# Two-layer hybrid encoder: memory values of the second layer split from an SBUF copy, memory key heads transposed and split later, rotation tables made from the twelfth slot on

## The chip, the core and the metric

The kernel runs on one core of one Trainium2 chip. The core has a matrix engine (TensorE, PE in the profile), a vector engine (VectorE, DVE), an activation engine (ScalarE, ACT), a general engine (GpSimd, POOL), and a queue for DMA issues (SyncE, SP). Each engine runs its own instructions strictly in the order in which the program lists them; between engines they wait for semaphores. The metric is device time of one execution in microseconds (us), lower is better.

## What is computed

```python
for i in range(DEPTH):                       # 2 layers, 512 tokens, width 1024
    h = rmsnorm(x, norm_g[i])
    mem_h = rmsnorm(mem, mem_norm_g[i])      # 256 memory tokens
    proj = jnp.einsum('bsd,de->bse', h, w_in)
    ...
    o_mem = memory_attention(q_mem, mem_h, w_mem_kv[i], mem_qn_g[i], mem_kn_g[i])
    y = jnp.concatenate([o_mix, o_mem], axis=-1) * jax.nn.silu(gate)
    x = x + jnp.einsum('bse,ed->bsd', y, w_out[i])

def memory_attention(q_mem, mem_h, w_kv, qn_g, kn_g):
    ...
    kv = jnp.einsum('bnd,de->bne', mem_h, w_kv).reshape(Bn, N, 2, MEM_HEADS, HEAD_DIM)
    k = rmsnorm(kv[:, :, 0], kn_g)
    v = kv[:, :, 1]
    s = jnp.einsum('bqhe,bkhe->bhqk', q, k).astype(jnp.float32)
    p = jax.nn.softmax(s, axis=-1).astype(v.dtype)
    return jnp.einsum('bhqk,bkhe->bqhe', p, v).reshape(Bn, S, MEM_W)
```

Layer 0 mixes tokens by dilated window attention, layer 1 by grouped-query attention whose queries and keys are turned by 2-D axial rotary tables. All arithmetic is in float32.

## The kernel before

**Three products for one.** A float32 matrix product is made of products of halves: an operand is cast to the type fp32r (the high half), and the rest, operand minus high half, is the low half. High times high, high times low and low times high are added up in PSUM. So everything that PE multiplies is first cast (mostly on ScalarE) and then subtracted (mostly on VectorE): two instructions on two engines, the second of which reads the first's result. For weights these are the lines 313 (`wh`) and 323 (`wo`), for the activations of the second layer 573 and 574.

**Seven products for eight.** `s_chunk` makes each block of 512 output columns in seven products instead of eight block products, with sums of the weights (in this layer all made by DMAs that add, issued on POOL, lines 278 to 297) and sums of the activations. The seven, in order: 12, 11, S1, S2, S4, S3, 22. Their activations, `h12`, `h11`, `hS1`, `hS2`, `hS4`, `hS3`, `h22`, are made at the end of the first layer from the residual stream, in two blocks of 128 tokens each (`diffs_t`, `rest_t`, whose `put` casts at line 573 and subtracts at line 574). PSUM banks are used twice: S2 adds on top of the bank of 11, after the addition at line 405 has read that bank out; S4 on that of 12, S3 on S2's, after a copy by line 388.

**Slots.** The order of work is written out by hand. A *slot* is one group of matmuls (12 of 512 columns in `mem_kv`, 24 of 256 in `s_chunk` here, about 2.9 us). In each slot the program lists: the matmuls of the group; `drv.free()`, the first step of whatever evacuates a bank that is due; `W.advance()`, the weights' work (line 323, a sum on POOL, line 313, loads on SyncE, in that order); `drv.tick()`, which first runs what was marked `soon`, then each waiting generator that is due (`yield n` puts it off by n slots), and then what was marked `late`. An instruction in a tick so stands behind the slot's own matmuls and ahead of those of the next slot.

The stretch around the change is the begin of the second layer. Its slots are called here:

- K1 to K4 and V1 to V4: memory keys and values, `mem_kv(1, ...)`, two halves of the contraction for two blocks of 128 memory tokens. They end about 661 us after the start.
- M1 to M7: the seven products of the memory queries, from 661 to 684.
- C1 to C7: those of the new keys and values, from 684 on; then come those of the queries, the gates, and the output.

The first slot, K1, has number 1, so that V1 is 5, M1 is 9, C1 is 16.

**What the change touches.** In `mem_kv`, `ev_k` squares the keys of a block in their bank (line 598), multiplies them by the reciprocal norm into an SBUF tile (line 603, in V1 and V2), transposes the four heads on PE two slots later (line 610, ticks V3 and V4), and splits the transposed heads in `put_norm`: the high half late in the same tick (line 647, ACT), the low half `LO_K[1]` = 5 slots on, at the begin of ticks M5 and M6 (line 650, DVE). `ev_v` splits the values straight from their bank: high half in V4 and M1 (line 675, ACT), low half at once for the first block and three slots on, in tick M4, for the second (line 678, DVE). `setup_b` loads the rotation tables and two gain rows by three DMAs on SyncE in tick `SET_B` = 9, M1, and multiplies them on VectorE in ticks M5, M6, M7 and C1 (four times line 1373, before the third of which line 1371 scales a gain). The tables are read first in tick C5 (lines 1430, 1431), the memory keys and values in the memory attention, which begins behind C7.

Squares, differences, copies of banks, `xn` and the tables' sources all take tiles of 128 x 512 from one pool of 14 buffers (`s2`). Weight loads (line 262) stand in SyncE's queue in the order in which the slots list them; SyncE runs ahead of the other engines as far as free buffers allow.

Of the kernel before, what the change touches and what calls it, by code (L numbers as in the profile page):

```python
# [10 lines left out]
F32 = mybir.dt.float32  # L11
F32R = mybir.dt.float32r
AF = mybir.ActivationFunctionType
ALU = mybir.AluOpType
# [7 lines left out]
TCKW = {}  # L22
NBIG, NM4, NS2, SCRATCH = 7, 23, 14, 2048
RING, LEAD = 4, 2
BULK, ACTIVE, SET_AT, MEM_B, PREP_Y, PREP_B, HALF, SET_B = 2, 2, 15, 14, 1, 1, {"a": 3, "b": 3, "o": 0}, 9
MEM_STEP = 1, 1
MEM_D = 4
DIRECT, DIRECT_B = (7,), (4, 5, 6, 7)
LO_K, LO_V = (9, 5), (0, 3)
PD = 2  # L30
EO = 2, 2, 1, 2, 2, 1
YB = {"m": (2, 2), "k": (1, 1, 1), 0: (1, 2, 1), 1: (1, 2, 1)}
# [98 lines left out]
def trunk_kernel(ctx: ExitStack, tc: tile.TileContext, x, mem, wall, norm_g, mem_norm_g, gcol,  # L131
                 qn_a, kn_a, qn_b, kn_b, ident_d, mask_d, tab_a, tab_b, out):
    nc = tc.nc
    V, A, G, T = nc.vector, nc.scalar, nc.gpsimd, nc.tensor
# [11 lines left out]
    def m4(dt=F32, name="m4"):  # L146
        return pool.tile([128, 1024], dt, tag="m4", name=name, bufs=NM4)

    def s2(dt=F32, name="s2"):
        return pool.tile([128, 512], dt, tag="s2", name=name, bufs=NS2)  # L150
# [350 lines left out]
    def turn4(src, hi, lo, mid=None):  # L501

        p = at("xT")
        for k in range(4):
            T.transpose(p[:, k * 128:(k + 1) * 128], src[:, k * 128:(k + 1) * 128], ident)
        p = p.rearrange("p (k t) -> p k t", k=4)
        if mid:
            mid()
        if hi is not None:
            split(hi, lo, p)  # L510
        return p
# [10 lines left out]
    def proj_t(act, sels, evac, mid=None):  # L522

        def group(w, u, b, p):
            for k in range(4):
                kk = 4 * u + k
                mm_early(p, sels[b](act, 0, kk), w[k][0], sels[b](act, 1, kk), w[k][0], kk == 0)
            if mid:
                mid(u, b)
            for k in range(4):  # L530
                kk = 4 * u + k
                mm_late(p, sels[b](act, 0, kk), w[k][1], kk == 7)
        chunk(2, len(sels), group, evac)
# [60 lines left out]
    def head_sq(p, n=4, by=QS):  # L594
        ss = sm(n, "hss")
        for j in range(n):
            jk = small.tile([128, 128], F32, tag="junk", name="junk", bufs=2)
            A.activation(jk, p[:, j * 128:(j + 1) * 128], AF.Square, scale=by, accum_out=ss[:, j:j + 1])  # L598
        return rstd_of(ss, n)

    def head_mul(p, r, n=4, dst=None):
        xn = (s2(name="xn") if dst is None else dst).rearrange("p (a b) -> p a b", a=4)
        V.tensor_tensor(xn[:, 0:n], p.rearrange("p (a b) -> p a b", a=4)[:, 0:n],  # L603
                        r[:, 0:n, None].to_broadcast([128, n, 128]), ALU.mult)
        return xn

    def transpose4(xn, n=4):
        p = at("qT")
        for j in range(n):
            T.transpose(p[:, j * 128:(j + 1) * 128], xn[:, j, :], ident)  # L610
        return p.rearrange("p (a b) -> p a b", a=4)
# [33 lines left out]
    def put_norm(q, gain, hi, lo, wait=0):  # L645

        drv.late(lambda: A.activation(hi, q, AF.Copy, scale=gain))
        if wait:
            yield wait
        drv.soon(lambda: V.scalar_tensor_tensor(lo, q, gain, hi.bitcast(F32), ALU.mult, ALU.subtract))  # L650
        yield 1

    def mem_kv(layer, M, mid=None):
        kt_ = [m4(F32R, "kmT").rearrange("p (h t) -> p h t", h=4) for _ in range(2)]
        vt_ = [m4(F32R, "vm").rearrange("p (b e) -> p b e", b=2) for _ in range(2)]

        def ev_k(b, p):
            r = head_sq(p) if layer else head_sq(p, by=rm[:, 2 + b:3 + b])

            def rest():  # L660
                if not layer:
                    G.tensor_scalar(r, r, rm[:, b:b + 1], None, ALU.mult)
                xn = head_mul(p, r)
                yield 2
                q = transpose4(xn)
                cs = slice(b * 128, (b + 1) * 128)
                yield from put_norm(q, gk_m[layer], kt_[0][:, :, cs], kt_[1][:, :, cs], LO_K[layer])

            drv.release(rest(), 2)
            yield 1  # L670

        def ev_v(b, p):

            h = 0.5 if layer else rm[:, 4 + b:5 + b]
            A.activation(vt_[0][:, b], p, AF.Copy, scale=h)
            if b and LO_V[layer]:
                yield LO_V[layer]
            V.scalar_tensor_tensor(vt_[1][:, b], p, h, vt_[0][:, b].bitcast(F32), ALU.mult, ALU.subtract)
            yield 1

        proj_t(M, NAT[:2], ev_k, mid)
        proj_t(M, NAT[:2], ev_v)
        return kt_, vt_

# [352 lines left out]
    p = turn4(mg[0, 0], None, None)  # L1037
# [631 lines left out]
```

## Time and profile before

| | |
|---|---|
| time, median of 3 runs | 953.63 us (952.09 to 953.82) |
| profiled execution | 953.29 us, of which span 951.4 us |
| PE busy | 937.2 us (99%) |
| VectorE busy | 790.0 us (83%) |
| ScalarE busy | 681.1 us (72%) |
| POOL busy | 340.0 us (36%) |
| granted TensorE clock | 1.00 |

How to read the lines that follow. In the stages, a row gives the stretch, its length, and for PE, its weight loads (PEld), DVE, ACT and POOL the busy time in it and the number of instructions, then the granted clock, the mean share of the DMA engines in use and the GB/s moved. In the order of time, a row gives start and length, engine, line, operation, out<-in, shape and count; in brackets how long the engine had been idle and what ended that. In PE's order, matmuls are pipelined and their ends are modelled, so that a row's length overlaps the next start; start to start is what it costs. A tile's rows give minimum, median and maximum in ns, and the first and last start. "DMA to landing" is from issue to the arrival of the data.

### The profile page before, as it was taken

To read this page: it belongs to the slowest core of one execution; us is meant where nothing else is said; L and a number is where in the kernel's file an instruction comes from. 1 tells how busy PE (TensorE), PEld (TensorE's weight loads), DVE (VectorE), ACT (ScalarE), POOL (GpSimd) and SP (SyncE) were. 2 spreads that over 40 slices of the span, in tenths; PEclk is the share of its full clock that TensorE was granted. 3 is DMA by queue.
4 is the path that set the end of the run, shared out by engine and by line. 5 is a ranking of instruction groups with operands and counts; after the bars stand their busy time and mean duration, and the time that the engine had idled before them with its cause. 6 is when DMAs were issued, how large, how long until landed. Compare 5 with 4: busy or idle time off the path is not lost.

```text
span 951.4 us, 16573 instructions
## 1 busy us (share of the span) xinstructions
PE 937.2 (99%) x5680; PEld 830.7 (87%) x5680; DVE 790.0 (83%) x1411; ACT 681.1 (72%) x1698; POOL 340.0 (36%) x484
## 2 busy tenths in 40 slices
PE   8999999999999999999999999999899999999998
PEld 6789888888888888888889998888899999998886
DVE  6997676878888888889798999868978998769982
ACT  7775689676868686868676768457778886878860
POOL 3323323656554545464827011213233241011110
PEclk9999999999999999999999999999999999999999
DMA  9999946869787878696868989979876686776524
GB/s 352 387 252 326 283 97 160 298 118 273 153 254 148 258 154 265 156 266 133 254 169 194 275 202 247 283 275 297 227 166 140 179 237 174 213 201 177 127 57 127
DMA packets 86198, 203.51 MB, mean 214 GB/s; under 512 B 25057, under 2 KB 34529, under 8 KB 86114
## 3 DMA queue, kind: packets, MB, share of 16 engines
q1 hardware_dynamic: 66962, 139.46, 42.9%
q0 software_dynamic: 17856, 60.83, 34.3%
q10 hardware_dynamic: 1296, 2.16, 0.6%
q8 instruction: 45, 0.74, 0.3%
q14 instruction: 39, 0.32, 0.1%
HBM read 156.48 MB, written 11.34 MB: 176 GB/s over the span
## 4 chain that ended last, share of the span: by engine, by line
PE 90%; DVE 4%; ACT 2%; DMA 2%; issue 1%; POOL 0%; SPq 0%; DVEq 0%; ACTq 0%; POOLq 0%
PE pj L176 24%; PE pj L175 24%; PE pj L179 24%; PE qT L610 2%; PE sa L1189 2%; PE oo L1297 2%; PE pt L1276 1%; PE ptb L1499 1%; DVE wo L323 1%; PE sa L1185 1%; PE ob L179 1%; DMA odb<-o 1%; PE pmt L735 1%; DMA m<-in_mem_dram 1%; PE ob L176 1%
## 5 line engine op out<-in xcount | busy, mean ns | idle before, releaser
L323 DVE TENSOR_TENSOR wo<-wl,wh 128x1024 fp32r<-128x1024 f32 x255 | 315.0, 1241 | 6.3 <-ACT wh L313 5.9
L313 ACT CAST wh<-wl 128x1024 fp32r<-128x1024 f32 x255 | 268.8, 1060 | 32.9 <-PE pj L176 19.2
L175 PE MATMUL pj<-wh,hS 128*128 128x512 f32 (+1 forms) x448 | 157.4, 365 | 1.7 <-DVE sn L405 1.7
L176 PE MATMUL pj<-wh,hS 128*128 128x512 f32 (+1 forms) x448 | 152.2, 353 | 0.6 <-DVE hS L574 0.6
L175 PE MATMUL pj<-wh,h 128*128 128x512 f32 (+1 forms) x336 | 117.8, 364 | 0.0
L176 PE MATMUL pj<-wh,h 128*128 128x512 f32 (+1 forms) x336 | 114.1, 353 | 1.1 <-DVE h L574 1.1
L453 POOL TENSOR_TENSOR rstd<-mse,half 128x4 f32<-128x4 f32 (+2 forms) x96 | 101.4, 1056 | 8.0
L179 PE MATMUL pj<-wo,hS 128*128 128x512 f32 (+1 forms) x448 | 99.9, 352 | 0.0
L175 PEld LDWEIGHTS pj<-wh,hS 128*128 128x128 f32 x448 | 84.8, 189 | 12.1 <-DVE sn L405 2.1
L176 PEld LDWEIGHTS pj<-wh,hS 128*128 128x128 f32 x448 | 84.9, 190 | 11.0 <-DVE hS L574 0.8
L179 PEld LDWEIGHTS pj<-wo,hS 128*128 128x128 f32 x448 | 74.7, 189 | 11.8
L452 POOL TENSOR_SCALAR mse<-hss 128x4 f32<-128x4 f32 (+1 forms) x86 | 42.6, 495 | 112.9 <-ACT junk L598 108.5
L388 ACT COPY sn<-pj 128x512 f32<-128x512 f32 x116 | 64.5, 590 | 24.0 <-PE pj L179 23.2
L1133 POOL TENSOR_TENSOR ta<-sn,tabs 128x128 f32<-128x128 f32 (+1 forms) x64 | 39.8, 629 | 116.6 <-DVE sn L603 91.1
L598 ACT ACTIVATE junk<-sn 128x128 f32<-128x128 f32 x264 | 79.2, 309 | 1.2 <-DVE sn L399 1.2
L179 PE MATMUL pj<-wo,h 128*128 128x512 f32 (+1 forms) x336 | 74.8, 352 | 0.0
L176 PEld LDWEIGHTS pj<-wh,h 128*128 128x128 f32 x336 | 63.7, 190 | 8.8 <-DVE h L574 1.3
L175 PEld LDWEIGHTS pj<-wh,h 128*128 128x128 f32 x336 | 63.6, 189 | 7.3
L405 DVE TENSOR_TENSOR sn<-pj,sn 128x512 f32<-128x512 f32 x87 | 59.6, 686 | 8.5 <-PE pj L179 8.1
L297 POOL DMA_DIRECT2D wl<-wl x33 | 29.5, 903 | 103.7 <-DVE wo L323 54.5
L179 PEld LDWEIGHTS pj<-wo,h 128*128 128x128 f32 x336 | 56.0, 189 | 8.8
L287 POOL DMA_DIRECT2D wl<-wl x33 | 31.3, 976 | 72.7 <-DVE wl L282 21.4
(252 smaller groups left out, 2363.6 us busy)
## 6 DMA issues: line engine op xcount, KB each, us to landing
wl<-in_wall_dram SPq DMA_DIRECT2D x222, 512.0 KB, 7.4
wl<-wl POOLq DMA_DIRECT2D x66, 512.0 KB, 6.2
wl<-in_wall_dram POOLq DMA_DIRECT2D x42, 512.0 KB, 8.6
od<-o SPq DMA_DIRECT2D x11, 256.0 KB, 5.7
og<-od SPq DMA_DIRECT2D x10, 256.0 KB, 9.4
x<-in_x_dram SPq DMA_DIRECT2D x4, 512.0 KB, 9.0
v0d<-sn SPq DMA_DIRECT2D x8, 256.0 KB, 8.4
acc<-in_x_dram POOLq DMA_DIRECT2D x8, 256.0 KB, 6.4
```

The costliest lines, as they stand in the source:

```text
L175: T.matmul(o, a, b, start=start, stop=False, skip_group_check=True)
L176: T.matmul(o, c, d, start=False, stop=False, skip_group_check=True)
L179: T.matmul(o, a, b, start=False, stop=stop, skip_group_check=True)
L287: G.dma_start(self.tile[key], self.tile[c, "T1", x], accum_op=ALU.add)
L313: A.copy(wh, self.tile[self.items[i]])
L323: V.tensor_tensor(wo, self.tile[key], wh.bitcast(F32), ALU.subtract)
L388: A.copy(t, b)
L405: V.tensor_tensor(t, b, t, ALU.subtract if q == "12" else ALU.add)
L452: G.tensor_scalar(e, ss, EPS, None, ALU.add)
L453: G.tensor_tensor(r, e, half[:, 0:n], ALU.pow)
L598: A.activation(jk, p[:, j * 128:(j + 1) * 128], AF.Square, scale=by, accum_out=ss[:, j:j + 1])
L1133: G.tensor_tensor(ta[:, 0:n], xn[:, 0:n, 0:32], ropeA[:, 0, b, s0:s0 + n], ALU.mult)
```

## The change

The first layer is left as it is. In the second layer:

- **Values.** ScalarE copies the scaled bank to an `s2` tile (`vr`) where it used to write the high half (V4 and M1). The high half is cast from that copy on ScalarE `HI_V` = 6 slots on (ticks M6 and M7), and the low half is subtracted on VectorE two slots behind that (ticks C1 and C2), now by a plain subtraction of two SBUF tiles. It adds one ScalarE instruction for each of two blocks.
- **Keys.** The transposes wait 6 slots instead of 2 (ticks M3 and M4 instead of V3 and V4), and with them the high halves; the low halves come 4 slots behind that instead of 5, at the begin of ticks C1 and C2 instead of M5 and M6.
- **Tables.** `SET_B` is 12 instead of 9: the three loads are issued in tick M4, and the products are made in ticks C1 to C4.

```diff
-BULK, ACTIVE, SET_AT, MEM_B, PREP_Y, PREP_B, HALF, SET_B = 2, 2, 15, 14, 1, 1, {"a": 3, "b": 3, "o": 0}, 9
+BULK, ACTIVE, SET_AT, MEM_B, PREP_Y, PREP_B, HALF, SET_B = 2, 2, 15, 14, 1, 1, {"a": 3, "b": 3, "o": 0}, 12
...
-LO_K, LO_V = (9, 5), (0, 3)
+LO_K, TURN_K, HI_V, LO_V = (9, 4), (2, 6), 6, (0, 2)
...
                 xn = head_mul(p, r)
-                yield 2
+                yield TURN_K[layer]
                 q = transpose4(xn)
...
         def ev_v(b, p):
 
             h = 0.5 if layer else rm[:, 4 + b:5 + b]
-            A.activation(vt_[0][:, b], p, AF.Copy, scale=h)
-            if b and LO_V[layer]:
+            if layer:
+                t = s2(name="vr")
+                A.activation(t, p, AF.Copy, scale=h)
+                yield HI_V
+                A.copy(vt_[0][:, b], t)
                 yield LO_V[layer]
-            V.scalar_tensor_tensor(vt_[1][:, b], p, h, vt_[0][:, b].bitcast(F32), ALU.mult, ALU.subtract)
+                V.tensor_tensor(vt_[1][:, b], t, vt_[0][:, b].bitcast(F32), ALU.subtract)
+            else:
+                A.activation(vt_[0][:, b], p, AF.Copy, scale=h)
+                V.scalar_tensor_tensor(vt_[1][:, b], p, h, vt_[0][:, b].bitcast(F32), ALU.mult, ALU.subtract)
             yield 1
```

## The prediction

> **What bounds the kernel now.** I read the page first, then the stages, then PE's, VectorE's and ScalarE's order of time around the change.
>
> ```profile
> span 951.4 us, 16573 instructions
> PE 937.2 (99%) x5680; PEld 830.7 (87%) x5680; DVE 790.0 (83%) x1411; ACT 681.1 (72%) x1698; POOL 340.0 (36%) x484
> 670.00:680.00 10.00, 8.77 (x71) 8.56 (x72) 10.00 (x15) 7.37 (x18) 3.09 (x4) 1.00 0.98 270
> 680.00:690.00 10.00, 8.94 (x75) 8.74 (x74) 9.86 (x15) 5.81 (x15) 2.56 (x3) 1.00 0.72 160
> ```
>
> TensorE (PE) is the bound, at a granted clock of 1.00: it is idle for 951.4 - 937.2 = 14.2 us, and only idle time on it can be won. In the two stages shown it idles 1.23 + 1.06 us, while VectorE (DVE) has not a free microsecond. These are M3 to M7, where the change works. The PE rows there:
>
> ```profile
> 660.65 0.60 PE L610 MATMUL qT<-ident,xn 128*128 128x128 f32 x4
> 661.01 0.36 PE L175 MATMUL pj<-wh,h 128*128 128x256 f32 x1
> ...
> 670.66 0.39 PE L175 MATMUL pj<-wh,hS 128*128 128x256 f32 x1 [0.79 <-DVE sn L405]
> ...
> 673.64 0.28 PE L175 MATMUL pj<-wh,hS 128*128 128x256 f32 x1
> ...
> 676.52 0.28 PE L175 MATMUL pj<-wh,hS 128*128 128x256 f32 x1
> ...
> 678.33 0.39 PE L176 MATMUL pj<-wh,hS 128*128 128x256 f32 x1 [0.57 <-DVE hS L574]
> ...
> 680.23 0.28 PE L175 MATMUL pj<-wh,h 128*128 128x256 f32 x1
> ...
> 682.53 0.39 PE L176 MATMUL pj<-wh,h 128*128 128x256 f32 x1 [1.06 <-DVE h L574]
> ...
> 684.43 0.28 PE L175 MATMUL pj<-wh,h 128*128 128x256 f32 x1
> ...
> 692.54 1.12 PE L179 MATMUL pj<-wo,hS 128*128 128x256 f32 x8
> ```
>
> M4 starts at 670.66, M5 at 673.64, M6 at 676.52, M7 at 680.23, C1 at 684.43. M5 runs undisturbed in 2.88 us. M4 waits for the addition that empties its bank (L405); M6 takes 3.71 and M7 4.20, because each waits halfway for the low half of its own activations (L574). All three waits end on VectorE. Its queue:
>
> ```profile
> L678 DVE SCALAR_TENSOR_TENSOR vm<-pj,vm x2: 683/686/689, 663.3 to 674.0; 128x512 fp32r<-128x512 f32 x2
> ```
>
> In order of time (start, length, and in brackets the idle time before it with its releaser):
>
> ```profile
> 665.84 0.69 DVE L574 TENSOR_TENSOR hS<-f,hS 128x512 fp32r<-128x512 f32 x1 [0.69 <-ACT hS L573]
> ...
> 669.92 0.69 DVE L405 TENSOR_TENSOR sn<-pj,sn 128x512 f32<-128x512 f32 x1
> ...
> 676.33 0.75 DVE L650 SCALAR_TENSOR_TENSOR kmT<-qT,gc,kmT 128x512 fp32r<-128x512 f32 x1
> 676.99 0.69 DVE L1373 TENSOR_TENSOR tabs<-tbraw,grB 128x512 f32<-128x512 f32 x1
> 677.59 0.69 DVE L574 TENSOR_TENSOR hS<-fS,hS 128x512 fp32r<-128x512 f32 x1
> ...
> 679.92 0.75 DVE L650 SCALAR_TENSOR_TENSOR kmT<-qT,gc,kmT 128x512 fp32r<-128x512 f32 x1
> ...
> 681.78 0.69 DVE L574 TENSOR_TENSOR h<-f,h 128x512 fp32r<-128x512 f32 x1
> ...
> 683.52 0.23 DVE L1371 TENSOR_SCALAR grB<-grB 128x128 f32<-128x128 f32 x1
> ...
> 687.53 1.22 DVE L323 TENSOR_TENSOR wo<-wl,wh 128x1024 fp32r<-128x1024 f32 x1
> ...
> 690.90 0.69 DVE L405 TENSOR_TENSOR sn<-pj,sn 128x512 f32<-128x512 f32 x1 [0.88 <-PE pj L179]
> ```
>
> Ahead of the three late instructions stand memory values (L678), memory keys (L650) and the rotation tables (L1373), none of which is used before C5. One of 512 elements takes 0.60 from start to start (676.99 to 677.59), an L650 0.66 (676.33 to 676.99). ScalarE (ACT), which feeds the L574s:
>
> ```profile
> 661.93 0.69 ACT L647 ACTIVATE kmT<-qT,gc 128x512 fp32r<-128x512 f32 x1
> 662.51 0.59 ACT L675 ACTIVATE vm<-pj 128x512 fp32r<-128x512 f32 x1
> ...
> 673.85 0.59 ACT L388 COPY sn<-pj 128x512 f32<-128x512 f32 x1
> 674.33 1.05 ACT L313 CAST wh<-wl 128x1024 fp32r<-128x1024 f32 x1
> 675.28 0.63 ACT L573 CAST hS<-fS 128x512 fp32r<-128x512 f32 x1
> ...
> 680.43 0.59 ACT L388 COPY sn<-pj 128x512 f32<-128x512 f32 x1 [3.06 <-PE pj L179]
> ```
>
> **M4: values' low half out of the way.** The first L678 (663.3) moves behind M7, so VectorE is 0.60 ahead. The idle 0.69 before 665.84 waits for a ScalarE cast; that cast comes earlier too, since an L647 leaves ScalarE in front of it (0.58, 661.93 to 662.51). The chain to L405 has no other gap: it runs at 669.32, and M4 starts at 670.06 instead of 670.66. PE itself would be ready earlier: 670.66 - 0.79 = 669.87, less 0.36 for the head transposes of which one pair, not two, now lies before M4 (660.65 to 661.01), gives 669.51. So M4 still waits for VectorE, about 0.55. Gain 0.60; the second head's 0.36 is still to be paid: 0.24.
>
> **M6.** M5 starts at 670.06 + 2.98 (M4's 670.66 to 673.64) + 0.36 = 673.40, M6 at 676.28. M6 ran dry 1.24 after its start (678.33 - 0.57 - 676.52), so it now needs its low half at 677.52. VectorE loses from its queue between 669.92 and 677.59 an L678, an L650 and an L1373, 1.86, and could be there at 675.13. It is not: ScalarE is now later. The key heads' copies (L647) run after M3 and M4; the second one needs transposes that start after M4 (673.04) and end 0.60 on, so it runs at 673.7. Then L388 at 674.28, L313 0.48 later, the cast 0.95 after that, 675.71, done at 676.33. L574 runs 676.38 to 677.07. M6 does not wait, with 0.45 to spare: gain 3.71 - 2.88 = 0.83.
>
> **M7.** It starts at 679.16 and needs its low half 1.24 later (682.53 - 1.06 - 680.23), at 680.40. From one L574 to the other VectorE took 4.19 (677.59 to 681.78), with an L650 and an L1373 in between; without them 2.93: 679.31 to 680.00. Gain 4.20 - 2.88 = 1.32, with 0.4 to spare. Sum at C1: 0.24 + 0.83 + 1.32 = **2.39 us**; C1 starts at 682.04.
>
> **Added copies.** A copy of values from SBUF on ScalarE isn't shown as such; the cast of an activation from SBUF (0.63, 675.28) is the same shape and is taken. Two of them stand in ticks M6 and M7, where ScalarE idles 3.06 before 680.43 and 4.2 of the ten from 680 (5.81 busy): nothing. Without that cover they would cost about 0.6 each. The copy that takes the place of L675 reads PSUM as L675 did (0.59). The values' low half now reads SBUF alone; L574, which does so too, and L678, from PSUM, both take 0.69, so I take no difference.
>
> **What is paid back in C1 to C4.** Before, VectorE came to the L405 that frees C4's bank at 690.90 after 0.88 idle, so it was free at 690.02. Now, between the L574 of M7 (2.47 earlier) and that L405 stand two L650 and two value subtractions more and one L1371 less: 2 x 0.66 + 2 x 0.60 - 0.26 (683.52 to the next table) = 2.26; of the tables two stand there before and after. It runs at 690.02 - 2.47 + 2.26 = 689.81 and is done at 690.50. C4 started some 0.96 after the row at 692.54, 693.50, and now at 691.11. It does not wait; the cover is 0.6 us, where it was 1.9. What is late next: L1371 and the last two tables, 0.26 + 2 x 0.60 = 1.46 more in C3 and C4. No PE instruction of these slots reads what stands behind them, and the first reader of a table is in C5. I take 0; the bound is 1.5, were PE to wait for all of it.
>
> **SyncE's queue.** The three table loads move from tick M1 to M4, past three weight loads. Its longest wait for the first of them, then seven weight loads and two of POOL's, each with its time to landing:
>
> ```profile
> SPq L1364 <- ACT sq L492: 4.3, 1, 4.3
> ...
> L262 SPq DMA_DIRECT2D wl<-in_wall_dram x7: 327/328/849, 651.1 to 660.8; - x7
> DMA to landing us min/median/max: 9.6/16.1/18.0
> ...
> 661.97 1.05 POOL L278 DMA_DIRECT2D wl<-in_wall_dram  x1
> DMA to landing us min/median/max: 12.1/12.1/12.1
> ...
> 675.35 0.93 POOL L287 DMA_DIRECT2D wl<-wl  x1
> DMA to landing us min/median/max: 6.6/6.6/6.6
> ```
>
> Now they wait for a buffer of a squared norm, long before M1. With the longest-free buffer handed out, as that row fits, the value copies take those two, and the tables get those of a difference last read in V4's tick and of the S4 block last read in M1's: VectorE leaves the first at 664.55 (the end of the instruction ahead of the idle 0.69 less 0.60) and the second somewhat before its L405 at 669.3. So SyncE stands until 669.3 at most, and behind it six weight loads, the last six of the row, which were issued by 660.8. They come 8 us later or more. Their first readers are an addition on POOL in C3 and casts from C5 on, behind the row at 690.90; even 18.0 after 671 that is in time, so I take 0. The bound above is the slow rival. Below 0: POOL's additions issued before 667 land sooner in an emptier queue; no PE wait hangs on them, so 0 too.
>
> **Time.** The profiled run took 953.29, its span 951.4 and 1.9 around it; the median shown is 953.63, the lowest 952.09. 953.29 - 2.39 = **950.9**. From C2 to the end PE's waits are these, 1.1 us in all, so the gain should reach the end:
>
> ```profile
> PE ob L179 <- DVE pbT L1508: 0.8, 1, 0.8
> PE ob L175 <- ACT pbT L1503: 0.3, 1, 0.3
> ```
>
> Bounds: M4's wait gone as well, 950.3; the margins of M6 and M7 missed, 951.7.
>
> **Rivals.**
> - *ScalarE takes VectorE's place.* One cast of weights (0.95, 674.33 to 675.28) later than reckoned, and M6 waits 677.07 + 0.95 - 677.52 = 0.5 and some 0.25 for its restart (before, 0.83 lost at 0.57 shown idle); M7 next to nothing. For: ScalarE has hardly any idle time from M1 to M5. Against: the margins of 0.45 and 0.4 hold by the rows. Gain 1.6: 951.7. With VectorE 1.2 late in C1 to C3 besides, C4 waits 0.6 more: 952.3.
> - *The gain is handed back.* In the attention PE, now ahead, meets a wait for VectorE or ScalarE that was hidden, as in the two rows above. For: the margins there are unknown. Against: the order there is unchanged and all engines shift together. Gain 0 to 1: 952.3 to 953.3.
> - *Slower: the bunched loads hold POOL's transfer.* L287, issued near 675.2 again, now meets the weight loads issued all at once. Its tile is cast in C1's slot and subtracted in C2's (the L323 at 687.53, now 687.53 - 2.47 + 0.66 + 0.60 - 0.26 - 0.60 = 685.5), ahead of the L405 for C4. It landed after 6.6. After 12.1, as L278 in M2, the cast ends at 688.4, VectorE is 2.9 late, C4 waits 2.3 and nothing is won. There it begins to decide: at 18.0, the longest of the weight loads, VectorE is 8.8 late, C4 waits 8.2 and the time is 959.1. For: some 3 MB start at once. Against: the DMA engines were as full before (0.98), and SyncE issues little from 652 to 667, so the crowd is moved, not added.
>
> How long L287 can take is the point of a rule of the Trainium skill (DMA: Bandwidth & Descriptors, the section Queues, rings and completion order): each DMA engine takes turns, packet by packet, between the queues that have work. By that a deep SyncE queue would at most double POOL's 6.6 to an estimated 13.2, C4 would wait 3.4, and the slow rival would end at 954.3 instead of 959.1. The 12.1 of L278 agrees; the bunch itself is in no trace yet.
>
> **Numbers.** Forecast 0.55; ScalarE 0.2; handed back 0.13; slower 0.12. Within 0.2%, 1.9 us, a measurement of this kernel can't tell a change from none. Faster by more: the forecast (2.4, less at its edge) and a little of the ScalarE case (1.6), 0.58; same: most of that case and the handed-back one, 0.29; slower 0.13. Range 949.8 to 954.0: the lower bound less 0.5, and up to the handed-back gain (953.3) plus the 0.3 to 0.5 by which the other runs shown at the upper end stand above the profiled one; this leaves out most of the slow rival.
>
> **What would show it.** Right: PE's waits before M6 and M7 gone, M4's at about 0.5, C1 near 682.0; no PE wait at C4; the table loads issued near 665 to 669 with six weight loads right behind. Wrong: the L573 ahead of M6's L574 ending after 676.8, a PE wait for L405 in C4, or L287 landing after 684. If M4's wait is unchanged, the value step is wrong; if M6's is, the key step.

## The result, and the profile after

The changed kernel took 951.0 us in the median of 9 runs (950.63 to 952.33), the kernel before 953.63 (952.09 to 954.32, 9 runs). The ratio is 0.9979, with a 95% interval of 0.9969 to 0.9989. So it is faster by 1.0 to 3.0 us, about 0.2%.

Three views of the changed kernel follow: two lines of the page of the profiled run (951.74 us), its stages (stretch, length, busy time and instructions of PE, PEld, DVE, ACT, POOL, then clock, DMA share, GB/s), and all that PE waited for from 640 us on (total, times, longest):

```profile
span 949.9 us, 16566 instructions
...
PE 938.8 (99%) x5680; PEld 833.0 (88%) x5680; DVE 790.4 (83%) x1411; ACT 681.5 (72%) x1700; POOL 337.5 (36%) x484
```

```profile
670.00:680.00 10.00, 9.33 (x79) 9.09 (x78) 8.88 (x13) 9.21 (x21) 4.30 (x4) 1.00 0.88 316
680.00:690.00 10.00, 10.00 (x86) 10.00 (x85) 8.87 (x13) 6.54 (x18) 2.54 (x3) 1.00 1.03 274
690.00:700.00 10.00, 9.81 (x82) 9.61 (x81) 9.97 (x15) 8.80 (x30) 8.09 (x10) 1.00 0.75 169
```

```profile
PE pj L175 <- DVE sn L405: 0.9, 2, 0.7
PE ob L179 <- DVE pbT L1514: 0.4, 1, 0.4
```

The two waits for L574 (M6 and M7) are gone, and VectorE has about 1.1 us free in each of the first two stages, where before it had next to none. PE idles 0.67 in the first (M4's wait, which is still there) and not at all in the second. A new wait stands in the third: L405 now ends two waits of PE, where it ended one. And the DMA engines, which before were fuller from 670 than from 680, are now fullest from 680 (1.03, before 0.72). In PE's order of time:

```profile
671.31 0.38 PE L175 MATMUL pj<-wh,hS 128*128 128x256 f32 x1 [0.67 <-DVE sn L405]
...
674.64 0.36 PE L175 MATMUL pj<-wh,hS 128*128 128x256 f32 x1
674.84 0.28 PE L176 MATMUL pj<-wh,hS 128*128 128x256 f32 x1
...
677.60 0.28 PE L175 MATMUL pj<-wh,hS 128*128 128x256 f32 x1
...
680.48 0.28 PE L175 MATMUL pj<-wh,h 128*128 128x256 f32 x1
...
683.36 0.28 PE L175 MATMUL pj<-wh,h 128*128 128x256 f32 x1
...
692.78 0.39 PE L175 MATMUL pj<-wh,hS 128*128 128x256 f32 x1 [0.19 <-DVE sn L405]
```

These are the starts of M4, M5 (with its second matmul), M6, M7, C1 and C4. This run came to the second layer 1.25 us late: V1 began at 648.74, in the profiled run of before at 647.49. Ahead of that the change touches nothing but the place of SyncE's loads, so slots are compared by their start after V1. Worked out from the PE rows of each kernel's profiled run, a second run of each kernel among them (us after V1):

| | M4 | M5 | M6 | M7 | C1 | C3 | C4 | C5 |
|---|---|---|---|---|---|---|---|---|
| before | 23.18 | 26.16 | 29.04 | 32.75 | 36.95 | 43.14 | 46.02 | 49.25 |
| before, second run | 23.18 | 26.15 | 29.03 | 32.73 | 36.94 | 43.13 | 46.01 | 49.25 |
| after | 22.57 | 25.90 | 28.86 | 31.74 | 34.62 | 40.81 | 44.04 | 47.37 |
| after, second run | 22.57 | 25.90 | 28.86 | 31.74 | 34.62 | 40.81 | 44.09 | 47.42 |

Two runs of one kernel agree within 0.05, so steps of a tenth can be read here, though whole times scatter by two. C1 comes 2.33 earlier. In C3 and C4 0.45 of it is lost again, and from C5 on 1.88 is left (1.83 between the second runs). Up to Q1, the first slot behind C7, nothing more changes.

The two profiled runs differ by 1.55: + 1.25 ahead of V1, - 1.88 in the changed stretch, and - 0.93 behind it (from Q1 to PE's last instruction 239.84, before 240.77). The last term isn't the change's either: the second run of before needs 239.98 there.

What takes the 0.45? VectorE's order of time in the changed kernel, from M6's L574 past the L405 for C4, then ScalarE's:

```profile
677.58 0.69 DVE L574 TENSOR_TENSOR hS<-fS,hS 128x512 fp32r<-128x512 f32 x1 [1.12 <-ACT hS L573]
...
680.52 0.69 DVE L574 TENSOR_TENSOR h<-f,h 128x512 fp32r<-128x512 f32 x1
...
687.77 1.23 DVE L323 TENSOR_TENSOR wo<-wl,wh 128x1024 fp32r<-128x1024 f32 x1 [1.03 <-ACT wh L313]
...
692.04 0.69 DVE L405 TENSOR_TENSOR sn<-pj,sn 128x512 f32<-128x512 f32 x1
...
695.78 0.68 DVE L1379 TENSOR_TENSOR tabs<-tbraw,grB 128x512 f32<-128x512 f32 x1
```

```profile
676.92 0.63 ACT L573 CAST hS<-fS 128x512 fp32r<-128x512 f32 x1
...
678.91 0.63 ACT L679 CAST vm<-vr 128x512 fp32r<-128x512 f32 x1
680.68 0.59 ACT L388 COPY sn<-pj 128x512 f32<-128x512 f32 x1 [1.14 <-PE pj L179]
...
682.11 0.62 ACT L679 CAST vm<-vr 128x512 fp32r<-128x512 f32 x1
...
686.70 1.05 ACT L313 CAST wh<-wl 128x1024 fp32r<-128x1024 f32 x1 [2.79 <-DMA wl<-wl]
```

Read backwards: C4's first matmul waits for L405; VectorE came to L405 late because it stood 1.03 at an L323 for a cast; ScalarE stood 2.79 at that cast (L313) for a DMA that adds to a weight tile. That is POOL's L287, and SyncE's queue shows what it met. Four views of the changed kernel follow: SyncE's order of time (issues of one line in a row are put together), what SyncE waited for (total, times, longest), the rows of the weight loads right behind the tables', and L287's row:

```profile
639.70 8.70 SPq L262 DMA_DIRECT2D wl<-in_wall_dram  x5
665.86 0.33 SPq L1370 DMA_DIRECT2D tbraw<-in_tab_b_dram  x1
668.94 0.33 SPq L1372 DMA_DIRECT2D grB<-in_qn_b_dram  x1
...
669.80 17.28 SPq L262 DMA_DIRECT2D wl<-in_wall_dram  x9
```

```profile
SPq L1370 <- DVE f L577: 17.4, 1, 17.4
...
SPq L1372 <- DVE hS L574: 2.7, 1, 2.7
```

```profile
L262 SPq DMA_DIRECT2D wl<-in_wall_dram x8: 328/400/688, 669.8 to 674.8; - x8
...
DMA to landing us min/median/max: 5.3/9.8/15.6
```

```profile
L287 POOL DMA_DIRECT2D wl<-wl x1: 926/926/926, 677.6 to 677.6; - x1
...
DMA to landing us min/median/max: 9.0/9.0/9.0
```

The tables' sources take buffers that VectorE frees only with its work of the ticks V4 and M1, just before 665.86 and 668.94, so SyncE stood 17.4 us at the first table load and 2.7 more at the second. Behind them eight weight loads went out between 669.8 and 674.8. L287, issued into that crowd, landed after 9.0 us, where it took 6.6 before.

### The profile page after: what moved, and what is told of

Its sections match the earlier page's. It is cut to its first block, busy times and chain, and to the rows that moved or that the text cites. A ratio compares the mean times of both kernels' runs of the same rounds, so it can differ in the third digit from the quotient of the medians.

```text
span 949.9 us, 16566 instructions
## 1 busy us (share of the span) xinstructions
PE 938.8 (99%) x5680; PEld 833.0 (88%) x5680; DVE 790.4 (83%) x1411; ACT 681.5 (72%) x1700; POOL 337.5 (36%) x484
## 4 chain that ended last, share of the span: by engine, by line
PE 94%; DVE 2%; DMA 2%; ACT 1%; issue 0%; SPq 0%; DVEq 0%; ACTq 0%
PE pj L175 25%; PE pj L176 25%; PE pj L179 24%; PE qT L610 2%; PE sa L1195 2%; PE oo L1303 2%; PE pt L1282 1%; PE ptb L1505 1%; PE sa L1191 1%; PE xT L505 1%; DMA wl<-wl 1%; PE ob L179 1%; PE ob L176 1%; PE ob L175 1%; PE sb L170 1%; PE sb L169 1%
## 5 line engine op out<-in xcount | busy, mean ns | idle before, releaser
L323 DVE TENSOR_TENSOR wo<-wl,wh 128x1024 fp32r<-128x1024 f32 x255 | 315.5, 1243 | 6.1 <-ACT wh L313 5.9
L313 ACT CAST wh<-wl 128x1024 fp32r<-128x1024 f32 x255 | 268.6, 1059 | 35.9 <-PE pj L176 18.7
L1139 POOL TENSOR_TENSOR ta<-sn,tabs 128x128 f32<-128x128 f32 (+1 forms) x64 | 37.6, 595 | 117.8 <-DVE sn L603 91.2
L405 DVE TENSOR_TENSOR sn<-pj,sn 128x512 f32<-128x512 f32 x87 | 59.6, 686 | 8.1 <-PE pj L179 7.8
L287 POOL DMA_DIRECT2D wl<-wl x33 | 31.2, 973 | 72.4 <-DVE wl L282 20.1
```

The source lines that it names most:

```text
L287: G.dma_start(self.tile[key], self.tile[c, "T1", x], accum_op=ALU.add)
L313: A.copy(wh, self.tile[self.items[i]])
L323: V.tensor_tensor(wo, self.tile[key], wh.bitcast(F32), ALU.subtract)
L405: V.tensor_tensor(t, b, t, ALU.subtract if q == "12" else ALU.add)
L1139: G.tensor_tensor(ta[:, 0:n], xn[:, 0:n, 0:32], ropeA[:, 0, b, s0:s0 + n], ALU.mult)
```

## The experiments

Every kernel is compared by its slots after V1. The times beside them are single runs unless said otherwise; their scatter (about 1 to 2 us) is larger than most steps. The second run of the kernel before took 953.58.

> The kernel before once more, to see what repeats. The three waits of PE in M4, M6 and M7 come from the order of VectorE's queue, so they should repeat to 0.05 us: 0.79, 0.57 and 1.06, and from the start of V1 to that of C1 36.95 us, to that of Q1 (first slot behind C7) 59.20. Open is the attention: from Q1 to PE's end it took 240.77 before the change and 239.83 after it, the difference being two waits near 862. If those waits belong to the order of the work, this run has 240.8 again; if they are chance, it lies elsewhere between 239.5 and 241.

Measured: waits of 0.79, 0.57 and 1.07, C1 at 36.94, Q1 at 59.19. From Q1 to PE's end it took 239.98, so the 240.77 of the first run does not come from the order of the work.

### Each part alone

The new values alone (before, with the change's `ev_v`):

```diff
-LO_K, LO_V = (9, 5), (0, 3)
+LO_K, HI_V, LO_V = (9, 5), 6, (0, 2)
...
+            if layer:
+                t = s2(name="vr")
+                A.activation(t, p, AF.Copy, scale=h)
+                yield HI_V
+                A.copy(vt_[0][:, b], t)
                 yield LO_V[layer]
...
+                V.tensor_tensor(vt_[1][:, b], t, vt_[0][:, b].bitcast(F32), ALU.subtract)
```

> The values' part alone. VectorE's order: M4 starts 0.60 earlier, because the first subtraction of values has left; the second has left ahead of M6, whose wait goes (0.83); M7 still waits, as key heads and tables stand ahead of its low half, 1.2. V1 to C1 36.95 - 1.4 = 35.5. If ScalarE set these times, its order here is that of before as far as M6, and nothing would be won: 36.9.

Measured: M4 22.87, C1 36.03, 952.64 us. M4 gained 0.31 only. VectorE's row ahead of M4's L405 says why, beside ScalarE's:

```profile
665.82 0.69 DVE L574 TENSOR_TENSOR hS<-f,hS 128x512 fp32r<-128x512 f32 x1 [0.98 <-ACT hS L573]
```

```profile
662.22 0.69 ACT L647 ACTIVATE kmT<-qT,gc 128x512 fp32r<-128x512 f32 x1
...
665.17 0.62 ACT L573 CAST hS<-f 128x512 fp32r<-128x512 f32 x1
```

VectorE is free earlier, but half of that goes into a longer wait for the cast (0.98, before 0.69), since the L647 still stands on ScalarE in M1. The key step has to take it away. M6 has no listed wait but takes 3.11, not 2.88: its low half (the L574 from 676.98 to 677.67) is done 1.17 after the slot's start, just too late. M7 takes 4.2 as before. So the forecast of 35.5 was missed, by half of M4's step and a quarter of M6's.

The later keys alone:

```diff
-LO_K, LO_V = (9, 5), (0, 3)
+LO_K, TURN_K, LO_V = (9, 4), (2, 6), (0, 3)
...
-                yield 2
+                yield TURN_K[layer]
```

> The keys' part alone. M4's wait stays (the values are still ahead of L405), though 0.7 us of head transposes leave from before it, so it shows as a longer wait, about 1.2 (0.79 and one pair of heads, 0.36). M6 and M7 lose an L650 each: M6 has no wait left, M7 0.2. V1 to C1 36.95 - 1.35 = 35.6. If key heads on ScalarE (two more copies between M3 and M5) hold up the casts, M6 waits longer than before and C1 comes no earlier than 36.9.

Measured: C1 35.63, 952.03 us. What PE waited for from 640 us on:

```profile
PE pj L175 <- DVE sn L405: 1.3, 1, 1.3
...
PE pj L176 <- DVE h L574: 0.2, 1, 0.2
```

M6's wait is gone and M7's is down to 0.2; M4's grows to 1.3, since PE, with the transposes out of the way, is there earlier.

The later tables alone:

```diff
-BULK, ACTIVE, SET_AT, MEM_B, PREP_Y, PREP_B, HALF, SET_B = 2, 2, 15, 14, 1, 1, {"a": 3, "b": 3, "o": 0}, 9
+BULK, ACTIVE, SET_AT, MEM_B, PREP_Y, PREP_B, HALF, SET_B = 2, 2, 15, 14, 1, 1, {"a": 3, "b": 3, "o": 0}, 12
```

> The tables' part alone. M4's wait stays at 0.79; M6 loses the one table ahead of its low half and does not wait; M7 still has the key heads of two slots ahead and waits 0.6. V1 to C1 36.95 - 1.3 = 35.65. The three parts alone then add up to 4.0, more than the 2.33 of all together: each wait can be removed once. The table loads, now behind a buffer that VectorE leaves near 662, hold SyncE here too; if this bunch of weight loads is what delays POOL's addition (9.0 us to landing after the change, 6.6 before), it should take more than 8 here as well.

Measured: C1 35.73, 951.28 us; PE's waits:

```profile
PE pj L175 <- DVE sn L405: 0.8, 1, 0.8
PE pj L176 <- DVE h L574: 0.5, 1, 0.5
...
```

M6's wait is gone here as well, and M7's is down to 0.5. L287 took 7.5, less than the bunch was expected to make of it; ScalarE waited 0.4 for it and PE not at all.

At C1 the three parts alone gain 0.92 + 1.32 + 1.22 = 3.46, together 2.33. Each takes instructions out of the one queue of VectorE, and a wait that one part has removed, as M6's, the others cannot remove again.

### Values and keys without the tables

The changed kernel, with the tables where they were:

```diff
-BULK, ACTIVE, SET_AT, MEM_B, PREP_Y, PREP_B, HALF, SET_B = 2, 2, 15, 14, 1, 1, {"a": 3, "b": 3, "o": 0}, 12
+BULK, ACTIVE, SET_AT, MEM_B, PREP_Y, PREP_B, HALF, SET_B = 2, 2, 15, 14, 1, 1, {"a": 3, "b": 3, "o": 0}, 9
```

> The changed kernel with the tables put back (loads in M1, products in M5, M6, M7 and C1). Theory: M4's gain needs two things, the values' subtraction off VectorE and the key copy off ScalarE ahead of it; the values alone brought 0.31 of the 0.60, because VectorE then waited 0.98 instead of 0.69 for ScalarE. Here both are gone, so M4 starts at 22.57 after V1, as after the whole change. The table of M5 falls into VectorE's 1.12 of idle time behind ScalarE, so M6 does not wait; the table of M6 makes the last low half 0.60 late against a margin of some 0.4: M7 waits 0.1 to 0.2. V1 to C1 34.62 + 0.3 = 34.9. Rival: the tables are a third of the gain, as alone (1.22): 35.4 or more. The table loads wait here for the buffers of V3 and V4, so SyncE still stands until about 665 and POOL's addition should land late, 8 us or more.

Measured: M4 22.57, M7 31.75, C1 35.03, C5 47.34, 951.79 us. M4 stands exactly as with the whole change, so values and keys together make that step, and M6 runs without a wait. The tables' part is M7: C1 comes 0.41 later without it. At C5 the two kernels are level (47.34 and 47.37): here C3 runs undisturbed in 2.88, and what the tables' move gains in M7 the whole change loses in C3 and C4. L287 took 8.5 here and ScalarE waited 2.9 for it, so the bunch does not come from the later tables alone. Nor does a late L287 alone cost PE anything: VectorE comes to the L323 in question at 39.39 after V1 here, when the cast is done (39.14); with the change it came at 38.00 and waited 1.03. SyncE's longest wait in this kernel:

```profile
SPq L1370 <- DVE f L577: 20.8, 1, 20.8
```

With the loads where they were, it is the value copies above all that leave them without a free buffer: with the values alone the first table load goes out at 658.36, with the keys alone at 647.67. Beside it, a second run of the changed kernel (950.56 us; its slots are in the table above):

> The changed kernel once more. What comes from the order of work repeats: V1 to C1 34.62, V1 to Q1 57.32, L287 9.0 to landing, C4's wait 0.19. What does not repeat is chance: V1's own place (648.74) and the stretch from Q1 to PE's end (239.84), which lay anywhere from 239.8 to 240.8 in the kernels so far.

Measured: C1 34.62, Q1 57.36, L287 9.0, C4's wait 0.24; V1 at 647.53, and 239.81 from Q1 to PE's end.

### The loads early, the products late

The changed kernel, with the three loads issued in tick V3 and the products still made in ticks C1 to C4:

```diff
-BULK, ACTIVE, SET_AT, MEM_B, PREP_Y, PREP_B, HALF, SET_B = 2, 2, 15, 14, 1, 1, {"a": 3, "b": 3, "o": 0}, 12
+BULK, ACTIVE, SET_AT, MEM_B, PREP_Y, PREP_B, HALF, SET_B = 2, 2, 15, 14, 1, 1, {"a": 3, "b": 3, "o": 0}, 7
...
-        yield 4
+        yield 9
```

> The changed kernel with the three table loads issued in tick V3 instead of M4; the tables' products stay in C1 to C4. If the six weight loads that stood behind the table loads made POOL's addition (L287) land late, and that made ScalarE's cast wait 2.79, VectorE 1.03 and PE at C4 0.19, then here SyncE runs ahead as before, L287 lands after 6 to 7 us, the cast does not wait and C3 takes 2.9 instead of 3.23: V1 to C5 47.37 - 0.4 = 46.95. If C4 is late only because VectorE got more work in C1 to C3, C3 stays at 3.2 and V1 to C5 at 47.4.

Measured: C1 34.61, C4 43.69, C5 46.92, one time of 952.05 us. SyncE's order and L287's row:

```profile
643.27 0.33 SPq L1370 DMA_DIRECT2D tbraw<-in_tab_b_dram  x1
...
644.84 39.65 SPq L262 DMA_DIRECT2D wl<-in_wall_dram  x13
```

```profile
L287 POOL DMA_DIRECT2D wl<-wl x1: 925/925/925, 678.3 to 678.3; - x1
...
DMA to landing us min/median/max: 4.8/4.8/4.8
```

The thirteen weight loads now spread over 39.65 us, L287 lands after 4.8, nobody waits for it, C3 runs in 2.88, and the 0.45 is back. The work that the change piles up on VectorE in C1 to C4 is all still there, so that work alone costs PE nothing. The late DMA alone cost nothing either, with values and keys; the 0.45 needs both, and taking the late DMA away is enough. All kernels line up by when SyncE gets past the table loads to the next weight load. At 14.9 us after V1 or later, L287 took 7.5 to 9.0 (14.9: tables alone 7.5, values alone 8.6; 17.9: values and keys 8.5; 21.1: the change, 9.0 in both runs). At 0.9 or earlier, it took 4.8 to 6.6 (0.9: keys alone 4.9, the kernel before 6.6 and 6.5; here, 4.6 ahead of V1, 4.8). SyncE waits for a buffer in all of them; what matters is when. L405 for C4:

```profile
691.57 0.68 DVE L405 TENSOR_TENSOR sn<-pj,sn 128x512 f32<-128x512 f32 x1
```

V1 is at 649.40 in this run, the latest of all; the time of 952.05 says nothing of the step.

### Both head transposes in one slot

The changed kernel, with the second block's transposes a slot earlier, so that both pairs lie before M4's wait and not one of them behind it:

```diff
-                yield TURN_K[layer]
+                yield TURN_K[layer] - (b if layer else 0)
```

> The changed kernel with both pairs of head transposes in the tick of M3, ahead of M4, where PE waits 0.67 for VectorE; after the change one pair stood there and one behind M4. If M4's start is set by VectorE's L405 alone, M4 starts as before relative to V1 (22.57), its wait falls to 0.3, and M5 and all behind it come 0.36 earlier: V1 to C1 34.62 - 0.36 = 34.26. If ScalarE, which gets the second key copy one slot earlier, is what binds there, M5 or M6 waits instead and C1 stays at 34.6.

Measured: M4 22.57, M5 25.55, C1 34.40, C5 46.79, one time of 950.18 us. PE's waits:

```profile
...
PE pj L175 <- DVE sn L405: 0.2, 1, 0.2
```

M4 starts when it did, its wait filled by the transposes; M5 comes 0.35 earlier and, with no transposes ahead of it, takes 2.88, not 2.96. At C1 0.22 is left: M6 takes 3.03 and M7 2.94, not 2.88. M6 halts for a moment halfway, where in VectorE's order the L574 of its low half has only just run:

```profile
676.79 0.28 PE L175 MATMUL pj<-wh,hS 128*128 128x256 f32 x1
676.97 0.39 PE L176 MATMUL pj<-wh,hS 128*128 128x256 f32 x1
```

```profile
676.22 0.69 DVE L574 TENSOR_TENSOR hS<-fS,hS 128x512 fp32r<-128x512 f32 x1 [1.09 <-ACT hS L573]
```

From matmul to matmul it takes 0.18 there, not 0.12, and VectorE in turn had waited 1.09 for ScalarE's cast. The margin of M6 is used up. Further on this edit gains what it was not made for. L287 takes 9.0 again and ScalarE waits 3.1 for it, but C3 runs in 2.88. VectorE's order says why:

```profile
682.03 1.41 DVE L650 SCALAR_TENSOR_TENSOR kmT<-qT,gc,kmT 128x512 fp32r<-128x512 f32 x2
...
686.51 1.22 DVE L323 TENSOR_TENSOR wo<-wl,wh 128x1024 fp32r<-128x1024 f32 x1 [0.48 <-ACT wh L313]
```

The second L650 of the keys now stands ahead of the L323 that waits for the cast, where with the change it stands behind it (688.92). So it fills half of VectorE's wait, 0.48 for 1.03, and L405 for C4 comes in time. Of the 0.45 about 0.1 is still paid, in C4. At C5 the edit gains 0.58.

Both edits together, in 11 runs:

> Both together, early table loads and both pairs of transposes behind M3: V1 to C5 47.37 - 0.4 - 0.36 = 46.6, and the time 951.0 - 0.75 = 950.2, ratio to the kernel before 0.9965 (the change alone: 0.9979). If the two gains hide each other, 950.6 or more.

Measured: C1 34.39, C5 46.69, so 0.68 earlier than with the change and 2.56 earlier than before. Alone, the two edits gain 0.58 and 0.45 at C5: they mostly win the same time, since the moved transposes leave the early loads (L287 4.8) only 0.1 to take away. The median is 951.23 (949.43 to 953.02), where 950.2 was expected; the ratio to the kernel before, 953.16 in 15 runs beside it, is 0.9979 (0.9969 to 0.9989). This is faster than before; that it is faster than the change the slots say and the times cannot: their interval is 1 us to each side.

## Why the prediction came out as it did

**M4.** Foretold 0.60 earlier with a wait of about 0.55 left; measured 0.61 and 0.67. The reason given has two halves, and both are needed: the values off VectorE, the L647 off ScalarE. Without the second, 0.31. The second pair of transposes was foretold to put 0.24 in place of 0.60 at M5; measured 0.26.

**M6 and M7.** Foretold gains of 0.83 and 1.32; both slots take 2.88 now, which is 3.71 - 2.88 = 0.83 and 4.20 - 2.88 = 1.32. Up to C1 it came to 2.33 for 2.39. What is missing lies in M5, which takes 2.96: its second matmul comes 0.20 behind the first (674.64 to 674.84), not 0.12, a restart behind the transposes that the sum left out. The chain named for M6, in which ScalarE and not VectorE decides, is the one that ran: with the 1.25 by which this run was later, the cast was to end at 677.58 and ended at 676.92 + 0.63 = 677.55; VectorE waited 1.12 for it. M7's L574 was to start at 679.31 + 1.25 = 680.56 and did at 680.52. One reading was off and did no harm: the prediction put the need for a low half at 1.24 after the slot's start, which is the modelled end of the ninth matmul. Where nothing waits, the tenth starts at 1.08 (in M6 from 677.60 to 678.68). By that the margins were 0.41 and 0.35.

**Copies.** The two added casts (L679, 0.63 and 0.62) stand where ScalarE had time left: it still idled 1.14 right behind the first, and 2.79 a few instructions behind the second. They cost nothing, as said.

**What is paid back in C1 to C4.** L405 for C4 was foretold at 689.81, which is 42.32 after V1. With the loads early it runs 691.57 - 649.40 = 42.17 after V1, and C4 doesn't wait. The last tables (695.78 the last) made PE wait nowhere. This step held; in the changed kernel itself something else came on top.

**SyncE's queue: here the prediction failed.** Place and buffers were right: loads foretold near 665 to 669 and issued from 665.86 on, with the weight loads right behind from 669.80, the wait for V4's difference first and for M1's S4 block next. The failing step is "so I take 0". It looked at the readers of the delayed weight loads and left L287, the transfer beside them, as fast as before; that case stood among the rivals only. The bunch was eight weight loads, where six were counted, and the term for L287 was the 6.6 of before; it measured 9.0, from an issue about 1 us later (677.64 - 648.74 = 28.90 after V1, before 675.35 - 647.49 = 27.86). VectorE stood 1.03 for it, and the cover of 0.6 at C4 that the prediction reckoned left 0.4 of that to pay: 0.45 was paid. Taken apart, C4 starts 0.35 later than with the loads early, and its second matmul comes 0.22 behind the first (692.78 to 693.00), not 0.12. Two of the prediction's own signs of being wrong showed, the wait for L405 in C4 and L287 landing after 684 (28.90 + 9.0 after V1, which is 685.4 in the run before). So the mechanism of the slow rival acts; its price was too high. It was to decide from 12.1 on, and this L287 took 9.0 at most, in all runs here.

How far it could go was put to a rule of the Trainium skill (DMA: Bandwidth & Descriptors, the section Queues, rings and completion order), by which a DMA engine takes turns between the queues that have work; from it the prediction estimated that a full SyncE queue at most doubles POOL's transfer. This L287 agrees: 4.8 with SyncE spread out, 9.0 with the bunch, and twice 4.8 is 9.6. The limit itself isn't shown: elsewhere in the changed kernel's profile other transfers of the same line take up to 12.0. The 6.6 on which the prediction built lies between the two.

**Time.** Foretold 953.29 - 2.39 = 950.9, measured 951.0. The agreement is closer than the working deserves. What the slots show of the change is 1.88, which from 953.29 makes 951.4; the medians differ by 2.6. The other 0.7 lies within the measurement (1.0 to 3.0 us), so that the sum and the median meet within 0.1 is luck.

**Rivals.** ScalarE in VectorE's place: out, M6 and M7 have no wait. Handed back in the attention: from Q1 to PE's end the changed kernel takes 239.84 and 239.81, the kernel before 240.77 and 239.98, so nothing was handed back. Slower: in a small size, as above.

## What to carry to other kernels

Work that nothing needs soon, but that stands in an in-order queue ahead of what the matrix engine waits for, can be moved, and the move can win its whole length there (0.60 at M4); look then at the second engine of the chain, which here had to be cleared too. A DMA that is moved needs a buffer that is free when its queue reaches it: otherwise the queue stands, and what it held back goes out at once, here just before another queue's transfer was due. Such a delay reaches the matrix engine only as far as the engines between have no other work to do first. Parts that clear the same queue don't add up.

## What the runs showed of the hardware besides

**Where a run begins its second layer.** V1 lies between 647.40 and 649.40 us in the eleven profiled runs, though all of them run the same program up to there except for the tables' loads. Four of them, those with V1 at 648.56 or later, share one mark, an early stretch with a granted clock of 0.96. The stretch and the wait in it, for the changed kernel's first run and, below, its second:

```profile
20.00:60.00 40.00, 37.60 (x179) 31.13 (x178) 36.27 (x49) 30.57 (x65) 14.53 (x24) 0.96 1.04 337
```

```profile
40.78 1.09 PE L505 MATMUL xT<-ident,x 128*128 128x128 f32 x4 [2.31 <-DVE fS L566]
...
42.10 0.63 PE L176 MATMUL pj<-wh,h 128*128 128x512 f32 x1
42.52 0.63 PE L175 MATMUL pj<-wh,h 128*128 128x512 f32 x1
```

```profile
40.13 0.63 PE L505 MATMUL xT<-ident,x 128*128 128x128 f32 x4 [2.33 <-DVE fS L566]
...
40.83 0.39 PE L176 MATMUL pj<-wh,h 128*128 128x512 f32 x1
41.06 0.39 PE L175 MATMUL pj<-wh,h 128*128 128x512 f32 x1
```

After the same wait of 2.3 us PE goes on at 0.42 from matmul to matmul in the one run (42.10 to 42.52) and at 0.23 in the other, and the slow pace lasts some 3 us. The kernel before shows both as well (1.00 in its first run, 0.96 in its second). What decides between them no run here shows. The seven runs without the mark have V1 at 647.40 to 648.26.

**PE's busy time.** The page gives PE 938.8 us busy after and 937.2 before, although it has the same 5680 matmuls; the second run of the changed kernel has 937.1. The 1.6 goes with the slow early stretch, and not with the change: the four runs that have it show 938.8 to 939.3 us, the other seven, before and after, 936.9 to 938.1.
